# Rotary embedding on one core: all stores on SyncE's ring, late loads on GpSimd's, one load behind a gate

## The chip, the core and the metric

The kernel runs on one core of a Trainium2 chip. The core has five engines that work side by side: TensorE (PE, matrix products), VectorE (DVE, elementwise work), ScalarE (ACT, activations and copies), GpSimd (POOL) and SyncE (SP, which only issues and waits). Data moves between the chip's memory (HBM) and the core's on-chip memory through 16 DMA engines. SyncE, ScalarE and GpSimd each have a queue (a ring) into these engines; a transfer that is issued on a ring is worked off after those issued on it before. The profile calls SyncE's ring q1, ScalarE's q10 and GpSimd's q0.

The metric is the device time of one execution in microseconds (us). The time before is 162.21 us, the median of 3 runs (162.07 to 162.32).

## The reference

The input x has the shape 16 (batch) x 512 (sequence) x 1024, in float32; a row of 1024 holds 16 heads of 64. In each head the first and the second half are rotated by tables over sequence position and index:

```python
x = x.reshape(batch, seq, num_heads, head_dim)
x1, x2 = x[..., :half_dim], x[..., half_dim:]
cos = cos[None, :, None, :]
sin = sin[None, :, None, :]
rotated = np.concatenate([x1 * cos - x2 * sin, x1 * sin + x2 * cos], axis=-1)
```

So each element is read once and written once: 33.55 MB in and 33.55 MB out, with two products and a sum for each.

## The kernel before

**Slabs.** The work is cut into eight slabs (`nslabs`) of two batches each. A slab is a tile of 128 partitions x 8192 float32 (4 MiB): each partition holds 8 whole rows (`rpp`). There are five buffers for slabs (`slots`, the pool `slabs`), and two buffers `xb` for a slab in bf16 (the pool `xpool`).

**Loads.** `load(s)` (line 60) takes the next buffer of the pool and issues the DMA that fills it. Slabs 0 to 5 are loaded through SyncE's ring, slabs 6 and 7 through GpSimd's. Slabs 0 to 4 are issued at the start; they need no wait, since each has a buffer of its own. After the store of slab s, `load(s + slots)` (line 150) issues slab s + 5, which takes over the buffer of an earlier slab. The framework that builds the program adds the waits: a load into a buffer that was used waits until the store out of it has landed.

**Tables.** cos and sin are loaded by two small DMAs on ScalarE's ring (line 76), cast to bf16 on GpSimd (line 97), spread over the partitions by eight matrix products (line 104) and copied to `tab` by VectorE (line 110).

**A slab's steps.** ScalarE casts the slab to bf16 (`cast`, line 119: `xb` from `slab`). VectorE makes a product with the sin part of the table (line 140; it goes into the slab's own buffer, seen as bf16), a product with the cos part in place in `xb` (line 140 again), and the sum of the two (line 143). ScalarE writes the sum back into the slab's buffer as float32 (line 146) and issues the store (line 148). Slabs 1 to 5 go through these steps whole, slabs 0, 6 and 7 in two halves (`passes`). The text calls the two copies on ScalarE the cast and the write-back.

**Order.** Each engine works through its instructions in a fixed order, which the framework's scheduler sets when the program is built; an instruction that waits holds up all that stand behind it on its engine. Before the change ScalarE's order is: cast of slab s + 1, write-back of slab s, store of slab s, and so on. VectorE takes the slabs one after the other.

Of the kernel before, what the change touches and what calls it, by code (L numbers as in the profile page):

```python
# [2 lines left out]

# [4 lines left out]


@with_exitstack  # L10
def kernel(
    ctx: ExitStack,
    tc: tile.TileContext,
    x: bass.AP,
    cos: bass.AP,
    sin: bass.AP,
    num_heads: int,
    out: bass.AP,
):
    nc = tc.nc  # L20
    P = nc.NUM_PARTITIONS

    batch, seq, dim = x.shape
    nh = num_heads
    hd = dim // nh
    half = hd // 2
    bf16 = mybir.dt.bfloat16
    f32 = mybir.dt.float32

    nb = 2  # L30
    slots = 5
    nslabs = batch // nb
    rpp = nb * seq // P
    W = rpp * dim
    SP = seq // rpp
    TW = rpp * half

    out_flat = out.rearrange("b s h d -> b s (h d)")

    singles = ctx.enter_context(tc.tile_pool(name="singles", bufs=1))  # L40
    slabs = ctx.enter_context(tc.tile_pool(name="slabs", bufs=slots))
    xpool = ctx.enter_context(tc.tile_pool(name="xpool", bufs=2))
    psum = ctx.enter_context(tc.tile_pool(
        name="psum", bufs=1, space=bass.MemoryType.PSUM))


    def dram(t, s, a=0, n=W):
        return bass.AP(tensor=t.tensor, offset=t.offset + s * nb * seq * dim + a,
                       ap=[[W, P], [1, n]])


    def view(t, offset, *dims):
        return dataclasses.replace(t, offset=t.offset + offset,
                                   ap=[t.ap[0], *[list(d) for d in dims]])


    slab = {}


    def load(s):  # L60

        queue = nc.sync if s < nslabs - 2 else nc.gpsimd
        slab[s] = slabs.tile([P, W], f32, tag="slab", name="slab")
        queue.dma_start(out=slab[s], in_=dram(x, s))  # L64


    load(0)


    KQ = 32  # L70
    QS = seq // KQ
    raw = singles.tile([P, 2 * QS * half], f32, tag="raw")
    for i, (eng, src) in enumerate(((nc.vector, cos), (nc.gpsimd, sin))):
        part = raw[:, i * QS * half:(i + 1) * QS * half]
        eng.memset(part, 0.0)  # L75
        nc.scalar.dma_start(out=part[::P // KQ, :], in_=bass.AP(
            tensor=src.tensor, offset=src.offset,
            ap=[[QS * half, KQ], [1, QS * half]]))

    for s in range(1, slots):  # L80
        load(s)


    NQ = QS // rpp
    pick = singles.tile([P, 2 * NQ * P], bf16, tag="pick")
    nc.gpsimd.memset(pick, 0.0)  # L86
    for g in range(2):
        for q in range(NQ):
            part = view(pick, (g * NQ + q) * P + q, (SP, P // SP), (NQ, KQ))
            nc.gpsimd.affine_select(  # L90
                out=part, in_=part, compare_op=mybir.AluOpType.not_equal,
                fill=1.0 - 2.0 * g, base=0,
                pattern=[[0, P // SP], [-(P // KQ), KQ]], channel_multiplier=1)

    tab1 = singles.tile([P, 2 * QS * half], bf16, tag="tab1")
    for i in range(2):
        nc.gpsimd.tensor_copy(out=view(tab1, i * QS * half, (1, QS * half)),  # L97
                              in_=view(raw, i * QS * half, (1, QS * half)))

    acc = psum.tile([P, 2 * rpp * hd], f32, tag="acc")  # L100
    for i in range(2):
        for h in range(2):
            for q in range(NQ):
                nc.tensor.matmul(  # L104
                    view(acc, i * rpp * hd + h * half, (hd, rpp), (1, half)),
                    view(pick, (i * h * NQ + q) * P, (1, P)),
                    view(tab1, i * QS * half + q * TW, (half, rpp), (1, half)),
                    start=q == 0, stop=q == NQ - 1)
    tab = singles.tile([P, 2 * rpp * hd], bf16, tag="tab")
    nc.vector.tensor_copy(out=tab, in_=acc)  # L110

    xb = {}


    def cast(u):
        s, r, n = u
        if r == 0:
            xb[s] = xpool.tile([P, W], bf16, tag="xb", name="xb")
        nc.scalar.copy(out=view(xb[s], r * dim, (1, n * dim)),  # L119
                       in_=view(slab[s], r * dim, (1, n * dim)))  # L120

    passes = []
    for s in range(nslabs):
        n = rpp if 1 <= s < nslabs - 2 else rpp // 2
        passes += [(s, r, n) for r in range(0, rpp, n)]


    cast(passes[0])
    for i, (s, r, n) in enumerate(passes):
        if i + 1 < len(passes):
            cast(passes[i + 1])
        xs = view(slab[s], r * dim, (1, n * dim))
        xu = view(xb[s], r * dim, (1, n * dim))

        t2 = view(slab[s].bitcast(bf16), 2 * r * dim, (1, n * dim))
        for t, a in ((t2, rpp * hd), (xu, 0)):
            nc.vector.tensor_mul(  # L140
                out=t, in0=xu,
                in1=view(tab, a + r * hd, (hd, n), (0, nh), (1, hd)))
        nc.vector.tensor_add(  # L143
            out=xu, in0=xu, in1=view(t2, half, (hd, n * nh), (-half, 2), (1, half)))

        nc.scalar.copy(out=xs, in_=xu)  # L146
        if r + n == rpp:
            nc.scalar.dma_start(out=dram(out_flat, s), in_=slab[s])  # L148
            if s + slots < nslabs:
                load(s + slots)  # L150


# [1 line left out]
_INS = ['x', 'cos', 'sin', 'num_heads']  # L154
_OUTS = [((16, 512, 16, 64), 'float32')]

_NUMBERS = {'num_heads': 16}


# [26 lines left out]
```

## Time and profile before

| what | value |
|---|---|
| median of 3 runs | 162.21 us (162.07 to 162.32) |
| the profiled execution, its own time | 162.06 us |
| its span | 160.3 us |
| VectorE busy | 109.0 us, 35 instructions |
| ScalarE busy | 113.6 us, 23 instructions |
| GpSimd busy | 4.4 us, 14 instructions |
| moved by DMA | 67.24 MB, mean 420 GB/s |
| a whole slab's cast, or write-back, on ScalarE | 7.02 us |
| a whole slab's product, or sum, on VectorE | 4.42 us |

The profiled execution lasts 1.76 us longer than its span, which runs from the first to the last thing that the profile shows. In the profile's lists of groups and of the timeline, a row has a line of the kernel, an engine, an operation, the tiles out and in with partitions x elements, and how often it occurs (x11). A row of the timeline begins with the start and the duration in us; what stands in brackets at its end is how long the engine had been idle and what ended that. The DMA row has 40 slices of the span, each digit the busy share in tenths, 9 for nine tenths or more. A row of a DMA queue gives its packets, the MB it moved, and the time of its packets as a share of the 16 engines' time.

### The profile page before, as it was taken

What the parts mean: (1) busy time and instruction counts of PE and PEld (TensorE: products, weight loads), DVE (VectorE), ACT (ScalarE), POOL (GpSimd) and SP (SyncE); (2) the same over time, 40 slices, a digit from 0 to 9 for tenths busy, and PEclk for the clock granted to TensorE, in tenths of its full rate; (3) what the DMA queues carried; (4) which work ended last, traced back from release to release, by engine and by line L of the source; (5) the groups of instructions that cost most, each with busy time, mean ns of one, the idle gap of its engine ahead of it and who ended that gap; (6) DMA issues with size and microseconds to landing.
All of it is one profiled execution on the core that took longest, in us unless ns stands there. A gap on an engine that the chain in (4) does not pass through costs nothing.

```text
span 160.3 us, 174 instructions
## 1 busy us (share of the span) xinstructions
PE 1.9 (1%) x8; PEld 1.1 (1%) x8; DVE 109.0 (68%) x35; ACT 113.6 (71%) x23; POOL 4.4 (3%) x14
## 2 busy tenths in 40 slices
PE   0004000000000000000000000000000000000000
PEld 0002000000000000000000000000000000000000
DVE  1000999999989979997996199939559599910000
ACT  3006939998998999899909995199995999280000
POOL 5002000000000000000010001000000000000000
DMA  7999999999999999999999999999999999999994
GB/s 245 417 418 393 499 417 393 474 433 401 384 401 417 474 417 393 474 442 393 458 458 393 450 466 393 433 474 401 417 458 433 393 474 442 393 458 458 393 450 204
DMA packets 2400, 67.24 MB, mean 420 GB/s; under 512 B 288, under 2 KB 288, under 8 KB 352
## 3 DMA queue, kind: packets, MB, share of 16 engines
q10 hardware_dynamic: 1248, 33.69, 48.7%
q1 hardware_dynamic: 864, 25.17, 37.4%
q0 software_dynamic: 288, 8.39, 12.1%
HBM read 33.69 MB, written 33.55 MB: 419 GB/s over the span
## 4 chain that ended last, share of the span: by engine, by line
DMA 49%; ACT 29%; issue 6%; DVE 4%; ACTq 0%; SPq 0%; POOLq 0%
DMA slab<-in_x_dram 28%; DMA out_dram<-slab 21%; ACT slab L146 16%; ACT xb L119 13%; DVE xb L143 1%; DVE xb L140 1%; DVE slab L140 1%; ACTq L148 0%; SPq L64 0%; POOLq L181 0%; ACTq L146 0%; POOLq L64 0%
## 5 line engine op out<-in xcount | busy, mean ns | idle before, releaser
L119 ACT CAST xb<-slab 128x4096 bf16<-128x4096 f32 (+1 forms) x11 | 56.6, 5155 | 24.9 <-DMA slab<-in_x_dram 23.6
L146 ACT CAST slab<-xb 128x4096 f32<-128x4096 bf16 (+1 forms) x11 | 56.6, 5153 | 3.5 <-DVE xb L143 3.5
L140 DVE TENSOR_TENSOR slab<-xb,tab 128x4096 bf16<-128x4096 bf16 (+1 forms) x11 | 35.9, 3260 | 15.4 <-ACT xb L119 15.3
L143 DVE TENSOR_TENSOR xb<-xb,slab 128x4096 bf16<-128x4096 bf16 (+1 forms) x11 | 35.9, 3261 | 0.3
L140 DVE TENSOR_TENSOR xb<-xb,tab 128x4096 bf16<-128x4096 bf16 (+1 forms) x11 | 35.9, 3261 | 0.3
L110 DVE CAST tab<-acc 128x1024 bf16<-128x1024 f32 x1 | 1.2, 1224 | 14.7 <-PE acc L104 14.7
L64 POOL DMA_DIRECT2D slab<-in_x_dram x2 | 1.2, 608 | 84.0 <-DMA out_dram<-slab 84.0
L119 ACT ACT_TABLE_LOAD x1 | 1.3, 1283 | 2.5 <-POOL pick L90 2.5
L104 PE MATMUL acc<-tab,pick 128*128 128x256 bf16 x8 | 1.9, 411 | 14.2 <-POOL tab L97 14.2
L97 POOL CAST tab<-raw 128x512 bf16<-128x512 f32 x2 | 1.2, 611 | 10.9 <-DMA raw<-in_cos_dram 10.9
L104 PEld LDWEIGHTS <-pick 128*128 128x128 bf16 x8 | 1.1, 136 | 14.5 <-issue 12.0
L75 DVE MEMSET raw<- 128x512 f32 x1 | 0.5, 485 | 0.9 <-PEq L167 0.9
L90 POOL TENSOR_SCALAR_AFFINE_SELECT pick<-pick 128x64 bf16<-128x64 bf16 x4 | 0.8, 250 | 0.1
L75 POOL MEMSET raw<- 128x512 f32 x1 | 0.5, 524 | 0.3 <-POOLq L167 0.3
L86 POOL MEMSET pick<- 128x512 bf16 x1 | 0.5, 525 | 0.0
L167 POOL MEMSET const-float32-0.0<- 128x1 f32 x1 | 0.1, 98 | 0.2 <-issue 0.2
L167 POOL MEMSET const-bfloat16-1.0<- 128x1 bf16 x1 | 0.1, 101 | 0.0
L167 POOL MEMSET const-uint8-127<- 128x1 uint8 x1 | 0.1, 101 | 0.0
L167 POOL MEMSET const-float32-1.0<- 128x1 f32 x1 | 0.1, 98 | 0.0
## 6 DMA issues: line engine op xcount, KB each, us to landing
out_dram<-slab ACTq DMA_DIRECT2D x8, 4096.0 KB, 26.8
slab<-in_x_dram SPq DMA_DIRECT2D x6, 4096.0 KB, 27.1
slab<-in_x_dram POOLq DMA_DIRECT2D x2, 4096.0 KB, 23.7
raw<-in_sin_dram ACTq DMA_DIRECT2D x1, 64.0 KB, 8.4
raw<-in_cos_dram ACTq DMA_DIRECT2D x1, 64.0 KB, 11.6
```

The source lines that it names most:

```text
L64: queue.dma_start(out=slab[s], in_=dram(x, s))
L75: eng.memset(part, 0.0)
L86: nc.gpsimd.memset(pick, 0.0)
L90: nc.gpsimd.affine_select(out=part, in_=part, compare_op=mybir.AluOpType.not_equal, fill=1.0 - 2.0 * g, base=0, pattern=[[0, P // SP], [-( ...
L97: nc.gpsimd.tensor_copy(out=view(tab1, i * QS * half, (1, QS * half)), in_=view(raw, i * QS * half, (1, QS * half)))
L104: nc.tensor.matmul(view(acc, i * rpp * hd + h * half, (hd, rpp), (1, half)), view(pick, (i * h * NQ + q) * P, (1, P)), view(tab1, i * QS * ...
L110: nc.vector.tensor_copy(out=tab, in_=acc)
L119: nc.scalar.copy(out=view(xb[s], r * dim, (1, n * dim)), in_=view(slab[s], r * dim, (1, n * dim)))
L140: nc.vector.tensor_mul(out=t, in0=xu, in1=view(tab, a + r * hd, (hd, n), (0, nh), (1, hd)))
L143: nc.vector.tensor_add(out=xu, in0=xu, in1=view(t2, half, (hd, n * nh), (-half, 2), (1, half)))
L146: nc.scalar.copy(out=xs, in_=xu)
L167: nc = _bacc.Bacc("TRN2", target_bir_lowering=False, num_devices=1)
```

## The change

Three things change. First, only slabs 0 to 3 are loaded through SyncE's ring, at the start; slabs 4 to 7 are loaded through GpSimd's. Second, slab 4 is no longer among the loads at the start: `load(4, gate=nc.vector)` is called in slab 1's turn, right after slab 1's sum, and before its DMA a memset on VectorE writes one column of the new buffer, so that the DMA has to wait for this memset. Third, all eight stores are issued by SyncE instead of ScalarE, behind the four loads on its ring. `load(s + slots)` is still called at the end of the turns of slabs 0, 1 and 2, and so load(5) is called at the end of slab 0's turn, ahead of load(4).

```diff
-    def load(s):
+    def load(s, gate=None):
 
-        queue = nc.sync if s < nslabs - 2 else nc.gpsimd
+        queue = nc.sync if s < slots - 1 else nc.gpsimd
         slab[s] = slabs.tile([P, W], f32, tag="slab", name="slab")
+        if gate is not None:
+            gate.memset(slab[s][:, :1], 0.0)
         queue.dma_start(out=slab[s], in_=dram(x, s))
...
-    for s in range(1, slots):
+    for s in range(1, slots - 1):
         load(s)
...
         nc.vector.tensor_add(
             out=xu, in0=xu, in1=view(t2, half, (hd, n * nh), (-half, 2), (1, half)))
+        if s == 1:
+            load(slots - 1, gate=nc.vector)
 
         nc.scalar.copy(out=xs, in_=xu)
         if r + n == rpp:
-            nc.scalar.dma_start(out=dram(out_flat, s), in_=slab[s])
+            nc.sync.dma_start(out=dram(out_flat, s), in_=slab[s])
             if s + slots < nslabs:
                 load(s + slots)
```

The scheduler sets the order anew for the changed program. On VectorE the memset stands between the two products of slab 3, and slab 5's first product between slab 4's second product and slab 4's sum. On ScalarE the write-back of slab 2 is followed by the write-back of slab 3 and then the casts of slabs 4 and 5; then come the write-back of slab 4, the first half cast of slab 6, and the write-back of slab 5. GpSimd issues the loads in the order 5, 4, 6, 7, behind the table casts.

## The prediction

> **What bounds the kernel now.** I read the page's first two parts, then its groups and issues, then the timeline of the engines, the chain, and at last the packets of single queues in chosen stretches. First the page, with engine totals, DMA slices, queues and issues:
>
> ```profile
> span 160.3 us, 174 instructions
> PE 1.9 (1%) x8; PEld 1.1 (1%) x8; DVE 109.0 (68%) x35; ACT 113.6 (71%) x23; POOL 4.4 (3%) x14
> DMA  7999999999999999999999999999999999999994
> ...
> HBM read 33.69 MB, written 33.55 MB: 419 GB/s over the span
> ...
> out_dram<-slab ACTq DMA_DIRECT2D x8, 4096.0 KB, 26.8
> slab<-in_x_dram SPq DMA_DIRECT2D x6, 4096.0 KB, 27.1
> ```
>
> The DMA engines are full from the first slice to the last but one, while VectorE and ScalarE have 51 and 47 us free. The kernel is bound by moving 67.24 MB: a change that keeps the queues fed can gain next to nothing, and one that lets the DMA engines run dry, or makes compute a serial chain, loses. So the question is which load comes how late, and what hangs on it. Next the timeline, for the start of the kernel, and for the two GpSimd loads:
>
> ```profile
> 13.56 1.17 POOL L97 CAST tab<-raw 128x512 bf16<-128x512 f32 x2 [10.94 <-DMA raw<-in_cos_dram]
> 13.61 7.11 ACT L119 CAST xb<-slab 128x4096 bf16<-128x4096 f32 x2 [9.81 <-DMA slab<-in_x_dram]
> 23.16 7.02 ACT L119 CAST xb<-slab 128x8192 bf16<-128x8192 f32 x1 [2.44 <-DMA slab<-in_x_dram]
> 28.70 2.29 DVE L143 TENSOR_TENSOR xb<-xb,slab 128x4096 bf16<-128x4096 bf16 x1
> ...
> 77.83 4.42 DVE L140 TENSOR_TENSOR xb<-xb,tab 128x8192 bf16<-128x8192 bf16 x1
> 80.09 0.69 POOL L64 DMA_DIRECT2D slab<-in_x_dram  x1 [65.36 <-DMA out_dram<-slab]
> ...
> 84.42 7.02 ACT L119 CAST xb<-slab 128x8192 bf16<-128x8192 f32 x1 [4.17 <-DMA slab<-in_x_dram]
> 91.35 7.01 ACT L146 CAST slab<-xb 128x8192 f32<-128x8192 bf16 x1
> 91.47 4.43 DVE L140 TENSOR_TENSOR slab<-xb,tab 128x8192 bf16<-128x8192 bf16 x1 [4.76 <-ACT xb L119]
> 95.93 4.42 DVE L140 TENSOR_TENSOR xb<-xb,tab 128x8192 bf16<-128x8192 bf16 x1
> ...
> 144.45 0.34 ACTq L148 DMA_DIRECT2D out_dram<-slab  x1
> ```
>
> Slab 0 lands at 13.6, slab 1 at 23.16, and slab 0's last sum is made at 31.0. Steps that follow each other take 6.93 us on ScalarE (84.42 to 91.35; 3.51 for half a slab, by the starts 103.77 and 107.28) and 4.46 on VectorE (2.33 for half). GpSimd is done with the tables at 14.73. Slab 7's store is issued at 144.45 and takes 15.0 to land, since it queues behind slab 6's; the span ends 0.8 later.
>
> How do two rings share the 16 engines? The packets of the queues from 85 to 103 us (name: packets, MB, share), with a GpSimd load beside ScalarE's stores:
>
> ```profile
> q10 hardware_dynamic: 133, 3.83, 49.3%
> q0 software_dynamic: 125, 3.93, 50.6%
> ```
>
> Evenly. Alone, the SyncE ring moved 4.23 MB from 23 to 33 us, so a slab of 4.19 MB takes 9.9 us alone and 19.8 beside another ring. From issue to landing the first load took 12.8: about 0.5 of issue, 1 to the first data, 9.9, 0.2 for the tables' bytes, and 1.2 until the slowest engine's last packet has landed.
>
> **The change, part by part.**
>
> *Who gets the spare buffer.* There are five slab buffers and now only four early loads. At the end of slab 0's turn the loop calls load(5), before slab 1's turn calls load(4) with the gate. So slab 5 takes the unused fifth buffer and waits for nothing; slab 4 takes slab 0's buffer and must wait for store 0. The built order says the same (slab_122 is slab 5, slab_129 slab 4, slab_78 slab 3):
>
> ```
> POOL 13 DMACopy slab_122<-in_x_dram
> POOL 14 DMACopy slab_129<-in_x_dram [waits DMAHW0,DMAHW6,DVE,Activation]
> DVE  15 TensorTensor slab_78<-xb_136,tab
> DVE  16 Memset slab_129 [waits DMAHW6]
> ACT  13-15 copies xb_145<-slab_129, xb_152<-slab_122, slab_129<-xb_145
> DVE  19-22 slab_129<-xb_145; xb_145<-xb_145; slab_122<-xb_152; xb_145<-xb_145,slab_129
> ```
>
> The gate thus stands behind slab 3's first product, not at slab 1's sum, and ScalarE now casts slab 4 and slab 5 before it writes slab 4 back.
>
> *Slab 5 early.* Its issue follows the table casts: 14.73, plus 0.6 of issue (0.69 and 0.53 in the trace), plus 1: data from 16.4. From there it takes half. Slab 1's data would have ended at 22.0 (23.16 less 1.2); the 5.6 us left become 11.2, so slab 1 lands at 28.8 instead of 23.16. Slab 5's remaining 4.3 take 8.6 more (data ends at 36.2), slab 2 lands at 43.0, slab 3 at 52.9 (data ends at 51.7).
>
> *The stores in SyncE's ring.* ScalarE: cast 1 28.8, write-back 0 35.7 and 39.2 (its sums, at 31.0, are no limit), store 0 issued at 42.8. It sits behind slabs 2 and 3 in the ring, starts at 51.7, ends at 61.6, lands at 62.8. The removed issues give ScalarE about 0.4 us each (37.23 to 37.62). None of them delays a later cast; SyncE takes over the eight issues (0.33 to 0.58 each for its loads) and waits for each store's write-back in turn; behind it stand only later stores, so that costs nothing while write-backs come in this order.
>
> *The gate.* Cast 2 43.0, write-back 1 49.95, cast 3 56.9, slab 3's first product 63.95, memset 68.4. Store 0 has landed 5.6 before, which is the cover of that wait; past 68.4 VectorE itself would stand, with slab 3's other two operations behind it. The memset of one column is not in the trace: I take 0.1, by GpSimd's 0.1 for 128x1, and at most 0.48 by VectorE's 128x512. It hides in VectorE's idle time before slab 4. Slab 4's load is issued at 68.5, data from 70.1. Slabs 6 and 7 queue behind it on GpSimd, each waiting for a store (1, 2) as before.
>
> *Slab 4's landing.* Store 1 ends at 71.5 (1.4 shared: 0.7 gained), store 2 (issued at 70.9) has data from 72.2 (0.7 alone), the other 8.5 take 17.0: data ends at 89.2, slab 4 lands at 90.4. Before, ScalarE was casting slab 4 at 66.3.
>
> *From there to the end*, a serial chain: cast 4, 7.05; slab 4's two products and, in between by the new order, slab 5's first, 3 x 4.46; slab 4's sum 4.43; 0.08; total 24.94. Then ScalarE back to back: write-back 4 (6.93), half cast of 6 (3.51), write-back 5 (6.93), half cast, write-back, half cast, write-back, each 3.51: 31.4, so 56.4 in all. Last half cast of slab 7 3.6, its three half operations 7.0 and gaps, last write-back 3.6: store 7 is issued 70.75 after the landing, at 161.15. It lands alone after 12.8 (by the first load; the ends are 12.4 with no table bytes and 15.0, the last store of before): 173.95, and 0.8 to the end: span 174.75. The DMA engines meanwhile run dry several times after 120 us, when slab 7 has landed; the cover that compute had before is gone.
>
> *The sum.* 174.75 against the profiled span 160.3 is +14.45; that execution took 162.06, 1.76 outside the span and 0.15 under the median 162.21. Predicted: 174.75 + 1.76 = **176.5**.
>
> *Bounds.* Slab 5 takes nothing from slabs 1 to 3: -5.0 (below). It is served alone at first: slab 1 at 33.1, +4.3. GpSimd's start: after the issue that ended at 80.78 the queue's first packets ended between 84.6 and 85.0, about 1.2 long, with two other rings in turn; so up to 2.7 instead of 1, +1.7. The gate's load shares less: at most -8.5, if store 2 stood back entirely. The last store: -0.4 to +2.2.
>
> *A rule against the row.* GpSimd issued a load in 0.69 us at 80.09 while VectorE ran a product from 77.83 to 82.25, so I add no wait for it. The Trainium skill, "SBUF — State Buffer", section "SBUF: two separate sides", holds that GpSimd's descriptor writing can be locked out while VectorE holds the port pair they share, until that instruction ends, and advises SyncE's or ScalarE's queues. By that rule slab 4's issue, under a 4.4 us product, would come up to 4.4 later and the sum would be 180.9 instead of 176.5.
>
> **The rivals.**
>
> 1. *Slab 5 does not delay slab 1* (SyncE's ring goes first while it has loads). For it: those loads were queued 12 us earlier. Against: the even share above. Then cast 1 is at 23.16 and the old pace holds: gate at 62.8, where store 0 lands (41.7 + 19.8 + 1.2, now sharing with slab 5), slab 4's data 64.4 to 84.2, landing 85.4. That is 5.0 less: 171.5. It holds from the point where slab 1 lands before 24.
>
> 2. *GpSimd's loads start late*, stuck behind VectorE's products or behind the other rings. For it: 3.8 us from an issue to the first packets' end. Against: the 0.69 us issue. Slab 4 comes later by up to one product, 4.42 us: 180.9.
>
> 3. *Not slower: slab 4 does get the spare buffer and opens at slab 1's sum*, as the change's words have it. For it: the sum of slab 1 ended at 39.82 + 4.42 = 44.2 in the trace, and slab 0 to 3 would then be the only early loads. Slab 4, issued at 44.3, has data from 45.9 and shares for 19.8 with stores 0 and 1: it lands at 66.9, about where ScalarE wanted it (66.32). The chain needs 70.75 + 12.8 + 0.8 = 84.35 after the landing, so anything before 75.95 leaves the DMA total as the bound: 162.2. Against: the order of the loads in the code and in the built program. Nothing in the profile lets slab 4 into slab 0's buffer before store 0 has landed (62.8), and from there it would have to load alone.
>
> **How the numbers follow.** My case 66 in 100, by itself 173.5 to 180; rival 1 14; rival 2 14; rival 3 3; other mixes, such as a ring order that hastens slab 4 over store 2, 3. Range 169.5 to 182: rivals 1 and 2 lie within, with the late last store and early slab 4 at its ends. This kernel's time can be told from no change by about 0.2%. Slower by more 0.97, within 0.02 (most of rival 3), faster 0.01.
>
> **What would show it.** The profile after should have: a GpSimd load issue at about 14.7, slab 1's cast at about 29 (rival 1: 23), the memset at about 68, slab 4's load issue just after it, its cast at about 90 with some 6 us of ScalarE idle before it, VectorE's sum of slab 4 after slab 5's first product, the last store issued at about 161, and DMA slices well below 9 in the last quarter. I am wrong if slab 4 is cast before 76, or if the memset waits for the store rather than for its place on VectorE.

## The result, and the profile after

The changed kernel takes 175.83 us (median of 6 runs, 175.63 to 176.8) against 162.24 before: a ratio of 1.085, with a 95% interval of 1.0824 to 1.0877. The change costs 13.6 us. The profiled execution took 175.63 us with a span of 173.8.

The page of the changed kernel, with the engines' totals, the DMA slices and their GB/s:

```profile
span 173.8 us, 188 instructions
PE 1.9 (1%) x8; PEld 1.1 (1%) x8; DVE 108.8 (63%) x36; ACT 113.5 (65%) x23; POOL 5.4 (3%) x16
DMA  7898999989999999999999999997598890992885
GB/s 241 385 483 377 475 430 415 475 377 475 415 347 445 437 407 483 369 422 407 445 430 407 400 452 422 437 445 309 241 483 362 362 483 0 407 437 121 347 377 241
HBM read 33.69 MB, written 33.55 MB: 387 GB/s over the span
```

VectorE and ScalarE do the same work as before, and the same 67.24 MB move. What changed is that the DMA engines stand still at times, all in the last third (one slice has 0 GB/s), where before they were full to the end. The timeline, from slab 1's cast to the last write-back, shows why (start and duration in us, engine, line, operation; the bracket gives the idle time before and its end):

```profile
14.66 0.69 POOL L66 DMA_DIRECT2D slab<-in_x_dram  x1
...
28.02 7.02 ACT L121 CAST xb<-slab 128x8192 bf16<-128x8192 f32 x1 [7.31 <-DMA slab<-in_x_dram]
...
68.03 0.06 DVE L65 MEMSET slab<- 128x1 f32 x1
68.12 4.42 DVE L142 TENSOR_TENSOR xb<-xb,tab 128x8192 bf16<-128x8192 bf16 x1
68.67 0.53 POOL L66 DMA_DIRECT2D slab<-in_x_dram  x1 [53.32 <-DVE slab L65]
...
91.12 13.94 ACT L121 CAST xb<-slab 128x8192 bf16<-128x8192 f32 x2 [7.01 <-DMA slab<-in_x_dram]
...
106.97 4.42 DVE L142 TENSOR_TENSOR slab<-xb,tab 128x8192 bf16<-128x8192 bf16 x1
111.31 4.42 DVE L145 TENSOR_TENSOR xb<-xb,slab 128x8192 bf16<-128x8192 bf16 x1
115.80 7.02 ACT L150 CAST slab<-xb 128x8192 f32<-128x8192 bf16 x1 [10.75 <-issue]
...
158.13 3.60 ACT L150 CAST slab<-xb 128x4096 f32<-128x4096 bf16 x1 [3.56 <-DVE xb L145]
```

The load issued at 14.66 is slab 5's, and slab 1 is cast at 28.02 instead of 23.16. The memset comes at 68.03, between slab 3's two products, and slab 4's load right after it. Slab 4 is cast at 91.12 (66.32 before); the row's second cast is slab 5's. Slab 5's first product (106.97) stands ahead of slab 4's sum (111.31), so slab 4's write-back starts only at 115.80. The chain that ended last (start, duration, engine, what) goes the same way:

```profile
56.60 7.03 ACT xb L121
63.63 0.02 issue
63.66 4.43 DVE slab L142
68.08 0.04 DVE slab L65
68.12 0.03 POOLq L66
68.15 0.52 issue
68.67 22.38 DMA slab<-in_x_dram
```

From slab 3's cast it passes through slab 3's first product and the memset into slab 4's load, and stays on compute from there until store 7. The DMA engines, which ended the kernel before, follow compute now. By stages (window, length, busy time of PE, PEld, VectorE, ScalarE and GpSimd, clock, DMA share, GB/s):

```profile
68.00:91.00 23.00, 0.00 (x0) 0.00 (x0) 8.94 (x4) 9.56 (x2) 1.06 (x2) 1.00 0.99 417
123.00:150.00 27.00, 0.00 (x0) 0.00 (x0) 21.28 (x10) 26.95 (x7) 0.00 (x0) 1.00 0.82 350
```

While slab 4 is on its way (68 to 91), VectorE and ScalarE are idle for most of the time, 14.1 and 13.4 of 23 us. From 123 to 150 ScalarE is full (26.95 of 27) and the DMA engines wait for it.

### The profile page after: what moved, and what is told of

Read it like the earlier page. It is cut to its first block, busy times and chain, and to the rows that moved or that the text cites. A ratio compares the mean times of both kernels' runs of the same rounds, so it can differ in the third digit from the quotient of the medians.

```text
span 173.8 us, 188 instructions
## 1 busy us (share of the span) xinstructions
PE 1.9 (1%) x8; PEld 1.1 (1%) x8; DVE 108.8 (63%) x36; ACT 113.5 (65%) x23; POOL 5.4 (3%) x16
## 2 busy tenths in 40 slices
DMA packets 2400, 67.24 MB, mean 387 GB/s; under 512 B 288, under 2 KB 288, under 8 KB 352
## 4 chain that ended last, share of the span: by engine, by line
DMA 36%; ACT 29%; DVE 17%; issue 10%; SPq 0%; ACTq 0%; POOLq 0%
DMA slab<-in_x_dram 36%; ACT xb L121 16%; ACT slab L150 12%; DVE slab L142 9%; DVE xb L142 4%; DVE xb L145 4%; SPq L66 0%; ACTq L150 0%; DVE slab L65 0%; ACTq L121 0%; POOLq L66 0%
## 5 line engine op out<-in xcount | busy, mean ns | idle before, releaser
L121 ACT CAST xb<-slab 128x4096 bf16<-128x4096 f32 (+1 forms) x11 | 56.5, 5154 | 24.8 <-DMA slab<-in_x_dram 24.7
L66 POOL DMA_DIRECT2D slab<-in_x_dram x4 | 2.3, 570 | 79.2 <-DVE slab L65 53.3
## 6 DMA issues: line engine op xcount, KB each, us to landing
out_dram<-slab SPq DMA_DIRECT2D x8, 4096.0 KB, 13.5
slab<-in_x_dram POOLq DMA_DIRECT2D x4, 4096.0 KB, 24.8
```

What stands on the lines that cost most here:

```text
L121: nc.scalar.copy(out=view(xb[s], r * dim, (1, n * dim)), in_=view(slab[s], r * dim, (1, n * dim)))
```

## The experiments

Two theories compete with the one of the prediction. Rival A: the stores' place behind the loads in SyncE's ring is what costs. Rival B: loads through GpSimd's ring are slow to start. All times are medians; the time before was 162.2 to 162.3 beside each run.

### Slab 4 early and ungated, rest as changed

```diff
-    for s in range(1, slots - 1):
+    for s in range(1, slots):
         load(s)
...
-        if s == 1:
-            load(slots - 1, gate=nc.vector)
```

> Edit: slab 4 is loaded among the early loads again, through GpSimd's ring and with no gate, so that it takes the spare fifth buffer and slab 5 takes slab 0's. Stores stay in SyncE's ring, slabs 4 to 7 in GpSimd's. Theory (slab 4 is late because slab 5 got the spare buffer and the gate held slab 4): slab 1 is still delayed to about 28 by the fifth early load, but slab 4 has landed at about 37, long before its cast at about 71, so the DMA engines stay busy and the time is 162 to 164. Rival A (stores behind the loads in SyncE's ring cost the time): it stays near 176. Rival B (loads on GpSimd's ring are slow to start): 170 to 176, since all four late loads are still there.

Measured: 165.4 us, a ratio of 1.0197 (1.0172 to 1.0222). Slab 1 is as late as in the changed kernel (cast at 27.96), stores and loads are in the same rings, and still 10.4 of the 13.6 us are gone. Rivals A and B are out as the main cause: what costs is that slab 4 is late, not which ring carries what. The theory missed by 1.4 us at the upper end, though, and 3.1 us stayed open; the last runs below settle them.

### The change as its words say it

Slab 4 gets a buffer of its own, and the memset is pinned behind slab 1's sum:

```diff
+    own = ctx.enter_context(tc.tile_pool(name="own", bufs=1))      # slabs: bufs=slots - 1
...
-        slab[s] = slabs.tile([P, W], f32, tag="slab", name="slab")
+        pool = own if s == slots - 1 else slabs
+        slab[s] = pool.tile([P, W], f32, tag="slab", name="slab")
         if gate is not None:
-            gate.memset(slab[s][:, :1], 0.0)
+            tc.keep_in_program_order(gate.memset(slab[s][:, :1], 0.0))
```

> Edit: slab 4 gets a buffer of its own and the other slabs share four; the gate's memset is pinned directly behind slab 1's sum on VectorE. This is the change as its words say it (rival 3 of the prediction). Theory: slab 1 is cast at about 23.2 again, the memset is at about 45, slab 4 shares the DMA engines with stores 0 and 1 and lands at about 67 to 69, just about when ScalarE wants it; time 162 to 167, at least 9 under the changed kernel. Rivals A and B: near 176, since the stores' ring and the loads' ring are unchanged.

Measured: 165.49 us, 1.0197 (1.0178 to 1.0216). The timeline of this run, the gate and slab 4's cast:

```profile
44.07 0.06 DVE L67 MEMSET slab<- 128x1 f32 x1
44.46 0.69 POOL L68 DMA_DIRECT2D slab<-in_x_dram  x1 [29.86 <-DVE slab L67]
68.69 7.02 ACT L123 CAST xb<-slab 128x8192 bf16<-128x8192 f32 x1 [3.54 <-DMA slab<-in_x_dram]
```

The gate opens at 44.07, as slab 1's sum ends, slab 4 is cast at 68.69, and the late chain is gone. So the prediction's third rival is what the change would have been with the spare buffer given to slab 4. Its time is again 165.5 and not the 162.2 that the prediction gave for it.

### The gate alone taken out

```diff
-            load(slots - 1, gate=nc.vector)
+            load(slots - 1)
```

> Edit: the memset alone is taken out; slab 4 still inherits slab 0's buffer and so waits for store 0, and slab 5 is still loaded early. Theory: slab 4's load is issued when store 0 has landed (about 62.5) instead of at 68.7, which is 6.2 earlier; it then has store 1 beside it for most of its time, lands at about 85 instead of 91, and the serial chain behind it is the same: 169 to 171. If the memset's place were no part of the cost: 176. If it were the whole cost: 162.

Measured: 172.64 us, 1.0636 (1.0609 to 1.0663). That is 3.2 less than the changed kernel, not 5 to 7. The load was issued where expected, but took longer. The rows of the timeline, then those of the DMA queues from 63.2 to 67.7 and from 67.7 to 68.7 (a row counts the packets that begin in its window):

```profile
63.19 0.53 POOL L66 DMA_DIRECT2D slab<-in_x_dram  x1 [48.04 <-DMA out_dram<-slab]
88.27 13.94 ACT L121 CAST xb<-slab 128x8192 bf16<-128x8192 f32 x2 [4.35 <-DMA slab<-in_x_dram]
...
q1 hardware_dynamic: 55, 1.80, 92.7%
...
q0 software_dynamic: 12, 0.39, 91.0%
q1 hardware_dynamic: 1, 0.03, 7.6%
```

From issue to the cast that waits for it, 25.1 us, where the prediction's terms give 22.5 (0.5 + 1 + 19.8 + 1.2). The excess lies at the start: until 67.7 only store 1's packets begin, so slab 4's data starts some 4.5 us after the issue and not 1.5. From there to the cast it takes 20.6, no more than the 21.0 of the terms. Slab 4 came 2.9 earlier than in the changed kernel (88.27 against 91.12), and the time followed it (3.2).

### Slab 5 held back until slab 3 has landed

```diff
+        if s == slots:
+            nc.gpsimd.tensor_copy(out=slab[s][:, :1], in_=slab[3][:, :1])
         queue.dma_start(out=slab[s], in_=dram(x, s))
```

> Edit: slab 5's early load is held back until slab 3 has landed (GpSimd first copies one column of slab 3 into the column that the load then overwrites); everything else as in the changed kernel, gate included. Theory: slab 1 is cast at 23.2 instead of 28.0, every step up to slab 3's first product comes 4 to 5 earlier, the memset is at about 63 to 65 (there store 0's landing, now sharing with slab 5, is close to being the limit), slab 4 lands at about 86.5 instead of 91.1: 171 to 173. If slab 5's share of the DMA engines were no part of the cost: 176.

Measured: 172.67 us, 1.0653 (1.0619 to 1.0687), as the theory said. Slab 1 is cast at 23.02 and the memset comes at 62.66, 5.4 earlier; slab 4's load is issued at 63.30 and slab 4 cast at 88.09. Of the 5.4 only 3.0 reach slab 4: in GpSimd's ring slab 5's load still stood before it, issued at 44.45 and landed at 68.7.

### The stores back on ScalarE's ring

```diff
-            nc.sync.dma_start(out=dram(out_flat, s), in_=slab[s])
+            nc.scalar.dma_start(out=dram(out_flat, s), in_=slab[s])
```

> Edit: the stores go back to ScalarE's ring; all else as in the changed kernel. The scheduler then puts the memset directly behind slab 1's sum, so VectorE itself stands there until store 0 has landed, and casts and write-backs alternate as before the change. Theory: store 0 now shares with slab 3 instead of waiting behind it and lands at about 62 all the same; slab 4's load is issued at about 62.5 instead of 68.7 and lands at 82 to 85; slab 4's sum no longer waits behind slab 5's product. VectorE loses some 13 at the gate (49 to 62), which it has to spare. Time 166 to 170. Rival A (the stores' ring is the cost): 162. Rival B (GpSimd's ring is the cost): near 176.

Measured: 167.73 us, 1.0343 (1.032 to 1.0367), inside the theory's 166 to 170 and away from both rivals. VectorE's timeline in this run:

```profile
43.73 4.43 DVE L145 TENSOR_TENSOR xb<-xb,slab 128x8192 bf16<-128x8192 bf16 x1
62.60 0.06 DVE L65 MEMSET slab<- 128x1 f32 x1 [14.44 <-DMA out_dram<-slab]
```

Here the scheduler put the memset directly behind slab 1's sum, and VectorE stood for 14.44 us until store 0 had landed: the wait that the prediction said was covered by 5.6 us in the changed kernel, seen uncovered. Even so the run is 8 us faster than the changed kernel. This experiment moves the ring, the memset and ScalarE's order together, so it does not price the ring. It does show that the ring did not hold up slab 0's buffer: store 0 landed at 62.5 here and at 62.6 in the changed kernel.

### Slab 4's sum ahead of slab 5's products

```diff
-            nc.vector.tensor_mul(
+            m = nc.vector.tensor_mul(
...
+            if s == slots:
+                tc.keep_in_program_order(m)
```

> Edit: only the order on VectorE is changed, by pinning slab 5's products behind slab 4's sum; the scheduler then also puts both half casts of slab 6 ahead of write-back 5. Theory (a serial chain behind the late slab 4): slab 4 lands at 91 as before, but its write-back starts 4.4 earlier, and with the half casts earlier the tail is packed closer by about 4: 171 to 173. If the DMA engines, not the chain, set the end: 176 as before.

Measured: 171.69 us, 1.0581 (1.0566 to 1.0597). The timeline after slab 4's late cast:

```profile
107.60 4.42 DVE L147 TENSOR_TENSOR xb<-xb,slab 128x8192 bf16<-128x8192 bf16 x1
111.94 4.42 DVE L142 TENSOR_TENSOR slab<-xb,tab 128x8192 bf16<-128x8192 bf16 x1
112.10 7.02 ACT L152 CAST slab<-xb 128x8192 f32<-128x8192 bf16 x1 [6.53 <-issue]
```

Slab 4 comes no earlier (cast at 91.63), its write-back starts at 112.10 instead of 115.80, and the time falls by 4.1 us. The scheduler also put both half casts of slab 6 (119.15) ahead of slab 5's write-back, so the 4.1 is the price of both orders together. No DMA was changed. That the kernel now ends on a chain of compute is shown by this run.

### Five loads early in SyncE's ring, stores behind them

```diff
-        queue = nc.sync if s < slots - 1 else nc.gpsimd
+        queue = nc.sync if s < slots else nc.gpsimd
```

(with the early load of slab 4 and without the gated one, as in the first experiment)

> Edit: slab 4 is loaded early through SyncE's ring as before the change (five loads there), slabs 5 to 7 through GpSimd's, all stores in SyncE's ring behind the five loads. Theory: store 0 is issued at about 37 but starts only at about 52, behind slab 4; all DMA work stays covered, slab 4 lands at about 52, slab 5 at about 85 as before the change: 161.5 to 164. Rival A (stores behind loads in one ring cost time): store 0 waits here 5 longer than in the changed kernel, so 170 or more.

Measured: 163.23 us, 1.0067 (1.0048 to 1.0085). Store 0, issued at 37.03, stands behind slab 4 and the rest of slab 3 and lands at 62.7, and the DMA slices are full to the end; Rival A's 170 is far off.

### The memset left to the scheduler, slab 4 with its own buffer

The second experiment without the pin.

> Edit: slab 4 gets a buffer of its own, and the memset is left to the scheduler. Nothing ties the memset to slab 1's sum but its place in VectorE's order, and with a free buffer the scheduler moves it to the very start, so slab 4 is loaded through GpSimd's ring from about 3 on and shares with slab 0. Theory: slab 0 lands at about 22 instead of 13.6 and slab 1 at about 33, everything on ScalarE starts 8 later, but the DMA engines never run dry: 162 to 165. If a late start of the compute were to be paid in full: about 170.

Measured: 165.81 us, 1.024 (1.0182 to 1.0298), 0.8 over the theory's end. The memset ran at 1.34 us, before any data had arrived:

```profile
1.34 0.06 DVE L67 MEMSET slab<- 128x1 f32 x1
1.73 0.66 POOL L68 DMA_DIRECT2D slab<-in_x_dram  x1
20.60 7.11 ACT L123 CAST xb<-slab 128x4096 bf16<-128x4096 f32 x2 [16.80 <-DMA slab<-in_x_dram]
```

The gate has no tie to slab 1's sum. It reads nothing of it; only its place in VectorE's order holds it, and that the scheduler chooses. Compute starts 7 us later here (20.60 against 13.61), and the time is still only 3.5 over the time before. ScalarE's end stands here in the same order as in the first experiment (both write-backs of slab 6 together, at 130.43), which took 165.4, so the late start itself seems to cost 0.4 at most; no run isolates it.

### Where the last 3 us lie

Three of these kernels end at 165.4 to 165.8. First, slab 4 early on GpSimd's ring with the stores back on ScalarE's, the first experiment's edit and the fifth's together:

> Edit: the run with slab 4 loaded early and ungated through GpSimd's ring (165.4), with the stores back in ScalarE's ring. It asks where the last 3 of the changed kernel's 13.6 lie. In that run slab 7 landed 3.5 later than before the change and both write-backs of slab 6 stood between the two half casts of slab 7, so that the last store was issued when the DMA engines had already run dry. Theory C (the scheduler's order at the end, which follows the stores' engine): slab 1 is still cast at 28, but casts and write-backs alternate again, the last store is issued while store 6 still moves: 162 to 163. Theory D (the early fifth load on GpSimd's ring, which delays slab 1): 165.4 as with the stores in SyncE's ring.

Measured: 162.33 us, 1.0007 (0.9993 to 1.0021): nothing is left, although slab 1 is still cast at 27.99. Theory D is out. Then the control for slab 5's ring, with slabs 0 to 4 early on SyncE's ring, 5 to 7 on GpSimd's and the stores on ScalarE's:

> Edit: the kernel before the change with slab 5 alone moved from SyncE's ring to GpSimd's (slabs 0 to 4 early on SyncE's, stores on ScalarE's). The run with the stores on SyncE's ring besides took 163.23 against 162.27. Theory: the ring of slab 5 does not matter, 162.0 to 162.5; the excess of the other run then lies in the stores' ring and in the order that goes with it. If it lies in slab 5's ring: 163.2.

Measured: 162.34 us, 1.0003 (0.999 to 1.0016). GpSimd's ring costs nothing, for slab 5 here and for slab 4 in the run before. At last the ring and the order were separated: the first experiment, stores in SyncE's ring, with ScalarE's last instructions pinned as the code states them:

```diff
-        nc.scalar.copy(out=xs, in_=xu)
+        c = nc.scalar.copy(out=xs, in_=xu)
+        if s >= slots:
+            tc.keep_in_program_order(c)      # the same for the casts
```

> Edit: the run with slab 4 early on GpSimd's ring and the stores in SyncE's ring (165.4), with ScalarE's casts and write-backs of slabs 5 to 7 pinned in the order in which the code states them (as before the change: a half cast, a write-back, a half cast, a write-back). The run with the stores back on ScalarE's ring took 162.3, but changed ring and order together. Theory C (the order): slab 6's second write-back is no longer needed before slab 7's work in another order, store 6 and store 7 come earlier, the DMA engines do not run dry before the last store: 162 to 163.5. Theory E (the stores' ring itself): 165.4 stays.

Measured: 162.35 us, 1.0003 (0.9993 to 1.0012). ScalarE's timeline at the end, first with the scheduler's order (165.4):

```profile
126.66 3.60 ACT L121 CAST xb<-slab 128x4096 bf16<-128x4096 f32 x1 [5.34 <-DMA slab<-in_x_dram]
130.17 7.11 ACT L148 CAST slab<-xb 128x4096 f32<-128x4096 bf16 x2
137.19 3.60 ACT L121 CAST xb<-slab 128x4096 bf16<-128x4096 f32 x1
147.85 3.60 ACT L148 CAST slab<-xb 128x4096 f32<-128x4096 bf16 x1 [3.56 <-DVE xb L145]
```

then pinned (162.35):

```profile
121.17 3.60 ACT L150 CAST slab<-xb 128x4096 f32<-128x4096 bf16 x1
126.67 3.61 ACT L121 CAST xb<-slab 128x4096 bf16<-128x4096 f32 x1 [1.91 <-DMA slab<-in_x_dram]
130.19 3.60 ACT L150 CAST slab<-xb 128x4096 f32<-128x4096 bf16 x1
133.69 3.60 ACT L121 CAST xb<-slab 128x4096 bf16<-128x4096 f32 x1
144.36 3.60 ACT L150 CAST slab<-xb 128x4096 f32<-128x4096 bf16 x1 [3.42 <-DVE xb L147]
```

Slab 7 lands at the same time in both (126.66 and 126.67). With the scheduler's order both write-backs of slab 6 follow that landing and hold back slab 7's second half cast (137.19 against 133.69); the last write-back starts 3.5 later, and store 7 meets DMA engines that have run dry (one slice before it falls to 128 GB/s; pinned, none of the last ten but the very last is under 392). With the order pinned one of the two is done while ScalarE would wait for slab 7, at 121.17. The stores' ring is the same in both: Theory E is out.

The 3.1 us are not a part of what the change costs, though. In the changed kernel ScalarE's end already stands in the code's order:

```profile
133.28 3.60 ACT L121 CAST xb<-slab 128x4096 bf16<-128x4096 f32 x1
136.79 3.60 ACT L150 CAST slab<-xb 128x4096 f32<-128x4096 bf16 x1
140.29 3.60 ACT L121 CAST xb<-slab 128x4096 bf16<-128x4096 f32 x1
143.95 3.61 ACT L150 CAST slab<-xb 128x4096 f32<-128x4096 bf16 x1
147.46 3.60 ACT L121 CAST xb<-slab 128x4096 bf16<-128x4096 f32 x1
```

So the kernel to compare with it is the pinned one, which has the same rings and the same order at ScalarE's end. Between the two lie 13.5 of the 13.6 us (175.83 to 162.35), and what was edited is when and how slab 4 is loaded. The first experiment gave back only 10.4 because, with slab 4 early and the stores on SyncE, the scheduler chose an order that itself cost 3.1 (165.4 to 162.35). Slab 5's early load, the inherited buffer and the gate are parts of the 13.5. Taken alone, holding back slab 5 and leaving out the gate gave 3.2 us each, and the sum ahead of slab 5's products 4.1; these were not tried together, so whether they add up is open. The two ring moves cost nothing that these runs can tell. Of the 1.0 us that five early loads in SyncE's ring with the stores behind them cost (163.23), the order is the likely cause by analogy; it was not pinned in that kernel, so this is not shown. No version was faster than the kernel before.

## Why the prediction was right

It said 176.5 (range 169.5 to 182, slower), and 175.83 was measured. Step by step, predicted and in the trace of the changed kernel:

| step | predicted, us | trace, us |
|---|---|---|
| slab 1 cast | 28.8 | 28.02 |
| store 0 issued | 42.8 | 42.07 |
| slab 2 cast | 43.0 | 42.63 |
| slab 3 cast | 56.9 | 56.60 |
| memset | 68.4 | 68.03 |
| slab 4's load issued | 68.5 | 68.67 |
| slab 4 cast | 90.4 | 91.12 |
| store 7 issued | 161.15 | 161.76 |
| from that cast to that issue | 70.75 | 70.64 |
| store 7, issue to landing | 12.8 | 11.1 |
| span | 174.75 | 173.8 |

*Who gets the spare buffer* carried the forecast, and it was right: slab 5's load waited for nothing (14.66), and slab 4 was cast 24.8 us later than in the kernel before (91.12 against 66.32). With slab 4 early (the first experiment) or in a pool of its own, slab 4's load no longer waited for store 0.

*Slab 5 early.* The even share held once slab 5's data moved. From 19 to 27 us the packets of the two queues in the changed kernel (packets, MB, share) were:

```profile
q0 software_dynamic: 50, 1.64, 47.4%
q1 hardware_dynamic: 49, 1.57, 45.5%
```

Rival 1 (slab 1 before 24) is out, and holding slab 5 back brought slab 1 to 23.02, as that rival's arithmetic had it. What was mis-sized is the start: slab 5's first packet began at 18.5, not at 16.4, so slab 1 lost less and was cast at 28.02 instead of 28.8.

*The gate* stood where the order put it. Store 0 landed at 62.6, 5.5 us before the memset (predicted: 5.6), and VectorE had no wait there.

*The terms that were mis-sized.* Store 7 alone took 11.1, not the 12.8 of the first load: -1.7. Slab 4's cast came 0.7 late. Its load was to have data 1 us after the issue, share with the end of store 1, and share with store 2 from 72.2 on. The queues from 71.3 to 72.5 and from 72.5 to 73.9 show something else:

```profile
q0 software_dynamic: 16, 0.52, 105.5%
q1 hardware_dynamic: 16, 0.00, 0.8%
...
q0 software_dynamic: 17, 0.56, 114.5%
```

The data began only at 71.3, 2.6 us after the issue, when store 1's last packets had begun, and then had the DMA engines to itself until store 2's data came at 74.0. The sum has a slip here as well: it lets slab 4 share the last 1.4 us of store 1 and still ends store 1 at 71.5. Shared, those take 2.8 (to 72.9), slab 4 lands at 91.1, and the total is 177.2. So the landing was hit within 0.7 because a later start and a longer stretch alone partly made up for each other, and of the last store's -1.7 the landing's +0.7 took back a part (span 173.8 against 174.75). The path was forecast; that the number is so close is in part luck. One bound was misread too: the packets that the prediction lets end between 84.6 and 85.0 began then, so the start after that issue took 3.9 us and not 2.7.

*Rival 3*'s price of 162.2 was wrong by 3.3 us (165.49 measured, with slab 4's own buffer and the pinned memset). That kernel's ScalarE ends in the order of the first experiment (both write-backs of slab 6 together, at 130.28), which cost 3.1 there; it was not pinned in this run. The forecast itself had the changed kernel's own order in its chain.

*The rule against the row.* GpSimd issued slab 4's load at 68.67 in 0.53 us, and by 72.5 16 of its packets had begun (the rows above), the first at 71.3, while VectorE's product ran from 68.12 to 72.54. Slab 5's load, issued at 14.66 with VectorE idle until 16.11, took longer, 3.8 us, to its first packet. So the load did not wait for the product to end, and rival 2's 180.9 is out. Its other half, a late start behind the other rings, did happen, but slab 4 was cast 0.7 later than forecast for it, not 4.4. The Trainium skill, "SBUF — State Buffer", section "SBUF: two separate sides", also sets a condition that the prediction passed over: an operation of VectorE with two inputs keeps out only a GpSimd operation that reads that memory, unless it runs in a two-port mode. The measurement fits the page in that reading, and not the use that the prediction made of it; in which mode the product ran, no run here shows.

## What to carry to other kernels

Where the DMA engines are full from end to end, ask of an edit to loads and stores which load comes late and how much compute stands behind it in series; which ring carries what may be worth nothing. Look for who gets the free buffer: here it was the load called first, not the one that the change was about. Look in the built order for where a gate ends up: written behind slab 1's sum and left to the scheduler, it stood there in one of these kernels, between slab 3's products in others and at the very start in one more. And when issues move from a computing engine to another one, compare the order of that engine's remaining instructions as well, since in the first experiment the order cost 3 us with no instruction added.

## What was not expected of the hardware

A load that is issued on GpSimd's ring while another ring keeps the DMA engines full starts late: its first packet began 4.4 to 5.5 us after the issue in six runs (slab 4 with the gate taken out and with its own buffer and a pinned memset; slab 5 in the first experiment, in its pinned form, with five early loads in SyncE's ring and with the memset left to the scheduler), and it landed 24.2 to 25.0 us after it. In the changed kernel, where store 1 was just ending, it was 2.6. GpSimd's ring is not alone in this: in the kernel before, store 0 on ScalarE's ring, issued at 37.23 beside loads, had its first packet at 41.4. With the DMA engines idle, store 7's first packet began 0.8 us after its issue and the store landed in 11.1; the first load, nearly alone, landed in 12.8.
